# Layer 0's projections bound in issue order to the hops of each head's scan

## The chip, the core and the metric

The kernel runs on one NeuronCore of a Trainium2 chip. The metric is the device time of one execution in microseconds (us). The kernel before took 2446.84 us in the median of three runs (2445.88 to 2450.79).

## What is computed

A decoder step of two layers over 1024 prompt tokens and 8 x 8 sample tokens, 1088 columns in all, with a model width of 1024. Layer 0 is a gated DeltaNet mixer with 8 heads of 128 x 128, layer 1 a dilated window attention. The change lies in layer 0 alone. For each head the input is projected to q, k and v, each passes a causal convolution of 4 taps and a SiLU, and then the prompt's 16 chunks of 64 tokens (the kernel takes 8 chunks of 128) go through a recurrence:

```python
def causal_conv_silu(u, buf, w):
    ...
    for i in range(1, CONV_W):
        y = y + ext[:, i:i + L] * w[i]
    return jax.nn.silu(y), ext[:, L:]

def gated_delta_rule(q, k, v, g, beta, S0):
    ...
    sol = lax.linalg.triangular_solve(a_mat, rhs, left_side=True, lower=True, unit_diagonal=True)
    ...
    def step(S, xs):
        w_c, kcum_c, qk_c, qdec_c, kdec_c, gtot_c = xs
        u = w_c - jnp.einsum('bhck,bhkv->bhcv', kcum_c, S)
        o = jnp.einsum('bhck,bhkv->bhcv', qdec_c, S) + jnp.einsum('bhij,bhjv->bhiv', qk_c, u)
        S = S * gtot_c[..., None, None] + jnp.einsum('bhck,bhcv->bhkv', kdec_c, u)
        return S, o
```

## The kernel before

A framework schedules the program: the code calls the stages in an order, and a scheduler with a timeline of its own lays each engine's instructions in one line. `order_after(inst, first, reason)` (L116) adds a dependency that binds the issue order alone and has no semaphore. Between two instructions of TensorE (PE) it says that the one stands behind the other in PE's line.

`project()` (L121) makes one projection tile: three chunks of columns (384, 384 and 320), each of 24 products at L128 into one PSUM tile `pp`: 8 tiles of the width, times three pairs of a high and a low part (`whi`, `wlo` of the weights, `hh`, `hl` of the input). That is 72 products for a tile. Its callback does the convolution on ScalarE (ACT) and VectorE (DVE, `ca` at L72).

Layer 0's work on a head has four stages.

- `stage_k(h)` (L622) projects k and forms the chunk's triangular system `MT`: the decay `DT` is fetched from DRAM (L643), eight products at L655 give `kk`. The system's diagonal blocks of 32 x 32 go through DRAM into another layout (L696, L699, tile `Mi`), where DVE inverts them in a loop of 31 steps, each a product at L710 (`vtmp`) and a sum at L712 (`Vi`). The widths grow to 256. The result goes through DRAM once more (L714 `vsc`, L719 `Vt`).
- `stage_qv(h)` (L722) projects q and v.
- `stage_inverse(h)` (L759) builds the inverse of 128 x 128 out of these blocks: PE groups at L766, L773, L777, L782, L786 and L790 with copies on ACT and DVE between them, then L809 and L810 and the scaling at L812, which leave `kT` and `vn` ready for the scan.
- `stage_scan(h)` (L820) is a chain over the 8 chunks. The first chunk has one product on the chain, L899 (`sc<-vn,kdec`), and a copy at L904. Each of the 7 others has two: L896 (`sc<-S,kT`), then `w` on DVE, then L899 (`sc<-w,kdec`), then `S` on DVE. These 15 products of a head are its hops, listed in `head["hops"]`. The outputs at L907, L910 and L832 lie beside the chain.

The main loop goes over h, with scan(h), then qv(h+1), k(h+2) and inverse(h+1) issued behind it, so that the projections of later heads fill the chain's gaps as the scheduler thinks fit. Heads 6 and 7 have no such projections left or only some; there the gate projections `gate()` stand behind the scan. Those of head 7 are bound by `behind` (L935): their product n goes behind hop (n - 54) // 16.

Of the kernel before, what the change touches and what calls it, by code (L numbers as in the profile page):

```python
# [22 lines left out]
NH = 8  # L23
# [19 lines left out]
def kernel(ctx, tc, I, O):  # L43
# [70 lines left out]
    def order_after(inst, first, reason):  # L114
        tc.add_manual_dep(inst.ins, first.ins.name,
                          mybir.DependencyInfo(mybir.DependencyClass.NoSync, mybir.DependencyReason.SCHED_ONLY),  # L116
                          reason=reason)

    newest = [None]

    def project(w, hh, hl, cb, chunks=CHUNKS, each=None):  # L121
        whi, wlo = w
        for ci, (c0, cn) in enumerate(chunks):
            acc = pp.tile([P, 512], F32, name="pp")
            n = 0
            for k in range(KD):
                for a, b in ((whi, hh), (whi, hl), (wlo, hh)):
                    mm = PE.matmul(acc[:, :cn], lhsT=a[:, k, :], rhs=b[k][:, c0:c0 + cn],  # L128
                                   start=(n == 0), stop=(n == 3 * KD - 1))
                    if each:  # L130
                        each(mm)
                    n += 1
            newest[0] = mm
            cb(ci, acc)
# [275 lines left out]
    def gate(pool, wsrc, h, hh, hl, done, zo="zo", zt="zt", bufs=3, each=None):  # L410

        w = wsplit(wraw(wsrc))
        def load(ci):
            oT = pool.tile([P, 384], F32, name="zo", tag=zo, bufs=bufs)
            SY.dma_start(out=oT[:, :CHUNKS[ci][1]], in_=oscr[h][:, CHUNKS[ci][0]:sum(CHUNKS[ci])])
            return oT
        tiles = [load(0)]

        def cb(ci, acc):
            c0, cn = CHUNKS[ci]  # L420
            cs = slice(c0, c0 + cn)
            oT = tiles[0][:, :cn]
            if ci < 2:
                tiles[0] = load(ci + 1)
            th = pool.tile([P, 384], F32, name="zt", tag=zt, bufs=bufs)
            A.activation(out=th[:, :cn], in_=acc[:, :cn], func=AF.Tanh, scale=0.5)
            stt(th[:, :cn], th[:, :cn], 1.0, acc[:, :cn], ALU.add, ALU.mult)
            stt(oT, th[:, :cn], 0.5, oT, ALU.mult, ALU.mult)
            done(ci, cs, oT)
        project(w, hh, hl, cb, each=each)  # L430

    def z_split(h, oh, ol):
        def done(ci, cs, oT):
            A.copy(out=oh[h][:, cs], in_=oT)  # L434
            (G if ci == 1 else V).tensor_tensor(out=ol[h][:, cs], in0=oT, in1=oh[h][:, cs].bitcast(F32),  # L435
                                                op=ALU.subtract)
        return done
# [18 lines left out]
    def slot(name, dtype=F32, shape=None):  # L456
        t = big.tile([P, 9 * P if name[:2] == "vn" else 8 * P if name == "DT1" else T], dtype, name=name)
        return t[:, :8 * P].rearrange("p (c n) -> p c n", n=P) if shape else t
# [87 lines left out]
    def conv_tile(t, dst):  # L546
# [3 lines left out]
        def cb(ci, acc):  # L550
# [34 lines left out]
            else:  # L585
                stt(dst[:, c0:NP], th[:, :256], 1.0, ca[:, :256], ALU.add, ALU.mult)
                v1 = th[:, 259:347].rearrange("p (b x) -> p b x", x=11)[:, :, 0:8]
                v2 = ca[:, 259:347].rearrange("p (b x) -> p b x", x=11)[:, :, 0:8]
                stt(sview(dst[:, NP:]), v1, 1.0, v2, ALU.add, ALU.mult)
        project(w, hh, hl, cb)  # L590
        if t != 8:
            ada.pump(1)
# [334 lines left out]
    heads = [{} for _ in range(NH)]  # L927

    def stage(f, h):
        if h < NH:  # L930
            f(h, heads[h])
# [5 lines left out]
    def behind(mm):  # L937
# [2 lines left out]
            order_after(mm, heads[-1]["hops"][hop], "leaves room for the chain of the scan")  # L940
        count[0] += 1

    stage(stage_k, 0)
    stage(stage_qv, 0)
    stage(stage_k, 1)
    stage(stage_inverse, 0)
    for h in range(NH):
        stage(stage_scan, h)
        stage(stage_qv, h + 1)
        stage(stage_k, h + 2)  # L950
        stage(stage_inverse, h + 1)
        for i in GATED.get(h, ()):
            def store(ci, cs, oT, i=i):
                SY.dma_start(out=oscr[i][:, cs], in_=oT)
            a, b = PLACE[i]
            if i == 2 and h == NH - 1:
                oT = slot("vT")
                SY.dma_start(out=oT, in_=oscr[2])
            if i != 2 or h == NH - 1:
                oh[i], ol[i] = slot(a, F32R)[:, :T], slot(b, F32R)[:, :T]  # L960
            if i == 2 and h == NH - 1:
                A.copy(out=oh[2], in_=oT)
                G.tensor_tensor(out=ol[2], in0=oT, in1=oh[2].bitcast(F32), op=ALU.subtract)
                continue
            gate(sb, W0[:, 3072 + i * P:3072 + (i + 1) * P], i, hh, hl, store if i == 2 else z_split(i, oh, ol),
                 "xin", "ca", 2, behind if h == NH - 1 else None)
    ada.pump(100)

    l0b.close()
# [12 lines left out]
    def out_project(pool, layer, wout, resid, x1, oh, ol, post, chunks=CHUNKS):  # L982
        a, b = chunks[0][0], sum(chunks[-1])
        for j in range(KD):
            w = wsplit(wraw(wout[:, j * P:(j + 1) * P]))
            xr = pool.tile([P, WIDE], F32, name="xr", bufs=2)[:, :b - a]
            SY.dma_start(out=xr, in_=resid[j][:, a:b])
            gt = GTm[layer]

            def cb(ci, acc):  # L990
                c0, cn = chunks[ci]
                n = min(cn, NP - c0)
                stt(x1[j][:, c0:c0 + n], acc[:, :n], gt[:, j, 0:1], xr[:, c0 - a:c0 - a + n], ALU.mult, ALU.add)
                if n < cn:
                    s = sview(x1[j][:, NP:])
                    V.tensor_tensor(out=s, in0=sview(acc[:, n:cn]), in1=bc(gt[:, j, 1:9], NL), op=ALU.mult)
                    V.tensor_tensor(out=x1[j][:, NP:], in0=x1[j][:, NP:], in1=xr[:, NP - a:], op=ALU.add)
            project(w, oh, ol, cb, chunks)
            sq = pool.tile([P, WIDE], F32, name="sq", bufs=2)[:, :b - a]
            A.activation(out=sq, in_=x1[j][:, a:b], func=AF.Square)  # L1000
            if j == 0:
                qs = sq
            else:
                V.tensor_tensor(out=sq, in0=sq, in1=qs, op=ALU.add)
                qs = sq
            post(j)
        return qs
# [444 lines left out]
    for hp in range(4):  # L1452
        smd, vnew = [None] * NG, [None] * NG
        nmd = sd.tile([P, 4], F32, name="nmd", bufs=2)
        for g in (2, 1, 0):
            qTs, kTs, vTs = (sb.tile([P, 2, NS], F32, name=n, bufs=3) for n in ("qTs", "kTs", "vTs"))
            for a in range(2):
                h = 2 * hp + a
# [105 lines left out]
```

## Time and profile before

| | us |
|---|---|
| median of three runs | 2446.84 |
| the profiled execution's own time | 2428.75 |
| its span | 2427.0 |
| PE busy | 2282.0 |
| DVE busy | 1376.6 |
| ACT busy | 941.6 |
| GpSimd (POOL) busy | 260.4 |

The span runs from the first to the last instruction of the profiled execution. A matmul of float32 shows as two records, a product of L128 as one. The granted clock of PE (PEclk) is a share of full speed: 1.00 is 2.4 GHz, 0.50 is 1.2 GHz.

### The profile page before, as it was taken

The page shows a single profiled execution, that of the slowest core. Times are in us where ns is not written, and L with a number is a line of the kernel's source. Part 1 is how long each engine was busy: PE and PEld are TensorE (multiplying, and loading weights), DVE is VectorE, ACT ScalarE, POOL GpSimd, SP SyncE. Part 2 cuts the span into 40 slices and gives each one's busy share as a digit, 9 for nine tenths or more (in the row PEclk, how much of TensorE's full clock was granted, in tenths as well). Part 3 has the DMA queues.
Part 4 walks back from the last instruction along what each step waited for, and adds up shares of the span by engine and source line. Part 5 has one row for each costly group of instructions (what it writes and reads, how often), then busy time and mean ns, then how long its engine had stood idle before and what let it go on. Part 6 is the DMA issues. An engine that isn't in the chain of part 4 may idle for free.

```text
span 2427.0 us, 43290 instructions
## 1 busy us (share of the span) xinstructions
PE 2282.0 (94%) x16647; PEld 2147.1 (88%) x16647; DVE 1376.6 (57%) x3414; ACT 941.6 (39%) x2477; POOL 260.4 (11%) x418
## 2 busy tenths in 40 slices
PE   7799999999999999899999999899998999999997
PEld 5688788779889898799988999899998999999897
DVE  6678767866875437327643374633737337375334
ACT  6445444444544324333233432334323333225234
POOL 3213222222321102200000000000000000000000
PEclk9889889888989999799999999999999999999999
DMA  9223223233223355439732497744967349785634
GB/s 324 62 68 91 63 74 84 60 73 79 79 77 97 88 158 165 131 84 335 228 109 74 132 345 204 237 115 125 351 197 249 115 122 340 198 288 169 213 103 148
DMA packets 482255, 379.42 MB, mean 156 GB/s; under 512 B 46206, under 2 KB 457071, under 8 KB 482048
## 3 DMA queue, kind: packets, MB, share of 16 engines
q1 hardware_dynamic: 482048, 376.65, 51.4%
q8 instruction: 131, 2.15, 0.4%
q14 instruction: 76, 0.62, 0.1%
HBM read 322.31 MB, written 54.27 MB: 155 GB/s over the span
## 4 chain that ended last, share of the span: by engine, by line
PE 67%; DMA 13%; DVE 9%; issue 6%; ACT 3%; POOL 1%; SPq 1%; POOLq 0%; ACTq 0%; DVEq 0%
PE pp L128 46%; DMA DT<-gcscr 2%; PE ps L1182 2%; PE ps L1200 2%; DMA qb<-qscr 2%; PE sc L1400 2%; DVE pr L1351 1%; DMA kc<-in_cache_kv_w_dram 1%; DMA wraw<-in_a_w_in_dram 1%; PE ps L1146 1%; DMA out_kv_s_dram<-knew 1%; PE ps L1191 1%; DMA aw<-in_ada_w_dram 1%; PE ps L150 1%; DMA out_y_p_dram<-yn 1%
## 5 line engine op out<-in xcount | busy, mean ns | idle before, releaser
L128 PE MATMUL pp<-hh,whi 128*128 128x384 f32 (+1 forms) x2688 | 915.2, 341 | 12.2 <-DVE vT L1140 4.2
L128 PE MATMUL pp<-hl,whi 128*128 128x384 f32 (+1 forms) x2688 | 906.1, 337 | 1.3 <-POOL hl L211 1.3
L128 PE MATMUL pp<-hh,wlo 128*128 128x384 f32 (+1 forms) x2688 | 901.5, 336 | 1.2 <-DVE wlo L111 1.2
L128 PEld LDWEIGHTS pp<-hh,whi 128*128 128x128 f32 x2688 | 514.0, 191 | 25.5 <-DVE vT L1140 6.6
L128 PEld LDWEIGHTS pp<-hl,whi 128*128 128x128 f32 x2688 | 514.6, 191 | 9.1 <-issue 4.6
L128 PEld LDWEIGHTS pp<-hh,wlo 128*128 128x128 f32 x2688 | 512.9, 191 | 6.3 <-issue 2.7
L111 DVE TENSOR_TENSOR wlo<-wraw,whi 128x1024 fp32r<-128x1024 f32 x136 | 170.2, 1251 | 127.7 <-ACT whi L110 126.9
L110 ACT CAST whi<-wraw 128x1024 fp32r<-128x1024 f32 x144 | 150.6, 1046 | 235.2 <-PE pp L128 146.2
L1187 ACT ACTIVATE sm<-sm,stg 128x128 f32<-128x128 f32 (+1 forms) x192 | 86.6, 451 | 359.8 <-DVE stg L1185 317.5
L1351 DVE TENSOR_TENSOR pr<-kc,qb 128x1024 f32<-128x1024 f32 x128 | 154.9, 1219 | 89.9 <-DMA qb<-qscr 56.2
L1341 DVE TENSOR_REDUCE ST<-pr 128x8 f32<-128x1024 f32 x128 | 153.7, 1214 | 1.1
L435 POOL TENSOR_TENSOR ol<-zo,oh 128x384 fp32r<-128x384 f32 x9 | 9.2, 1017 | 1302.6 <-ACT oh L434 1285.7
L72 DVE SCALAR_TENSOR_TENSOR ca<-xin,cwT,ca 128x384 f32<-128x384 f32 (+1 forms) x216 | 130.4, 608 | 7.6 <-ACT ca L577 6.2
L1185 DVE CUSTOM_DVE_ANT_0 sm<-ps,mA 128x256 f32<-128x256 f32 (+1 forms) x128 | 48.3, 377 | 137.1 <-PE ps L1182 136.2
L1200 PE MATMUL ps<-vnat,pT 128*128 128x128 f32 x560 | 96.3, 279 | 4.4 <-DVE pT L1196 4.4
L710 DVE TENSOR_TENSOR vtmp<-Vi,Mi 128x2 f32<-128x2 f32 (+30 forms) x248 | 95.7, 386 | 4.4 <-PE ps L690 0.7
L1182 PE MATMUL ps<-kT,qT 128*128 128x128 f32 (+1 forms) x384 | 93.3, 324 | 3.8 <-DVE stg L1185 3.6
L1200 PEld LDWEIGHTS ps<-vnat,pT 128*128 128x128 f32 x560 | 85.6, 189 | 10.6 <-ACT pTn L1380 4.2
L1194 ACT COPY pT<-ps 128x256 f32<-128x256 f32 (+1 forms) x96 | 32.4, 337 | 114.7 <-PE ps L1191 113.5
L128 PE MATMUL pp<-oh,whi 128*128 128x384 f32 (+1 forms) x216 | 72.0, 333 | 2.7 <-DVE zt L72 2.7
L72 DVE SCALAR_TENSOR_TENSOR hh<-pp,GT,xr 128x384 f32<-128x384 f32 (+1 forms) x48 | 27.3, 571 | 83.0 <-PE pp L128 79.2
L1185 DVE CUSTOM_DVE_ANT_0 sm<-ps,mG 128x128 f32<-128x128 f32 x64 | 18.4, 288 | 98.6 <-PE ps L1182 69.1
(449 smaller groups left out, 3681.5 us busy)
## 6 DMA issues: line engine op xcount, KB each, us to landing
qb<-qscr SPq DMA_DIRECT2D x128, 512.0 KB
kc<-in_cache_kv_w_dram SPq DMA_DIRECT2D x104, 512.0 KB
vc<-in_cache_kv_w_dram SPq DMA_DIRECT2D x104, 512.0 KB
wraw<-in_b_w_in_dram SPq DMA_DIRECT2D x80, 512.0 KB
wraw<-in_a_w_in_dram SPq DMA_DIRECT2D x32, 512.0 KB
wraw<-in_ada_w_dram SPq DMA_DIRECT2D x24, 512.0 KB
stgc<-gscr SPq DMA_DIRECT2D x32, 260.0 KB
aw<-in_ada_w_dram SPq DMA_DIRECT2D x8, 1024.0 KB
```

Source lines behind the costliest of these rows:

```text
L72: return (eng or V).scalar_tensor_tensor(out=out, in0=in0, scalar=scalar, in1=in1, op0=op0, op1=op1)
L110: A.copy(out=hi, in_=raw)
L111: (eng or V).tensor_tensor(out=lo, in0=raw, in1=hi.bitcast(F32), op=ALU.subtract)
L128: mm = PE.matmul(acc[:, :cn], lhsT=a[:, k, :], rhs=b[k][:, c0:c0 + cn], start=(n == 0), stop=(n == 3 * KD - 1))
L710: V.tensor_tensor(out=tv, in0=Vi[:, :na, :w], in1=Mi[:, :w, c].unsqueeze(1).broadcast_to([P, na, w]), op=ALU.mult)
L1182: PE.matmul(sv, lhsT=qT[:, b * P:(b + 1) * P], rhs=kT[:, k0:k0 + w], start=True, stop=True)
L1185: V.tensor_tensor_reduce(out=sm[:, :w], in0=sv, in1=mk, scale=1.0, scalar=3e38, op0=ALU.add, op1=ALU.min, accum_out=stg[:, b, 128:129])
L1187: A.activation(out=sm[:, :w], in_=sm[:, :w], func=AF.Exp, scale=-1.0, bias=stg[:, b, 128:129], accum_out=stg[:, b, 129:130])
L1200: PE.matmul(ob[:, (b % 4) * P:(b % 4 + 1) * P], lhsT=pT[:, i * P:(i + 1) * P], rhs=vnat[:, k0 // P + i, :], start=(i == 0), stop=(i == w / ...
L1341: V.tensor_reduce(out=sv[:, n:n + 4, :], in_=pr.rearrange("p (n a e) -> p n a e", a=2, e=P), op=ALU.add, axis=AX.X)
L1351: V.tensor_tensor(out=out, in0=k, in1=q, op=ALU.mult)
L1400: mm = PE.matmul(od[32 * j:32 * j + 8, f * P:(f + 1) * P], lhsT=Z[g][:, a * NB + 2 * j + c, 8 * k:8 * k + 8], rhs=vc[:, j, a * P:(a + 1) * P],
```

## The change

`project()` gets a list of functions, `paced`, that each of its products is passed to when the caller gave none. `along(h)` makes such a function for head h: the product n of the projections issued beside that scan goes behind hop (n - 24) // 14 from n = 24 on (for head 6: (n - 48) // 24 from 48 on), and every later one behind the last hop at the latest. The list is set anew behind each `stage_scan(h)` and emptied at the end of the layer. Nothing is computed otherwise.

```diff
+    paced = []
+
     def project(w, hh, hl, cb, chunks=CHUNKS, each=None):
...
-                    if each:
-                        each(mm)
+                    for f in [each] if each else paced:
+                        f(mm)
                     n += 1
...
+    def along(h):
+
+        n, hops = [0], heads[h]["hops"]
+        step, free = (24, 48) if h == NH - 2 else (14, 24)
+
+        def each(mm):
+            if n[0] >= free:
+                order_after(mm, hops[min(len(hops) - 1, (n[0] - free) // step)], "along the chain of the scan")
+            n[0] += 1
+        return each
+
...
     for h in range(NH):
         stage(stage_scan, h)
+        paced[:] = [along(h)]
         stage(stage_qv, h + 1)
         stage(stage_k, h + 2)
         stage(stage_inverse, h + 1)
...
+    paced.clear()
     ada.pump(100)
```

The scheduler lays all engines anew with these bounds, up to the end of layer 0. In the changed program the lines from L122 on stand 2 further down.

PE, the inverse of the head to come: before, it is laid between the hops of the running head. Here L773 and L777 are groups of the inverse of head 3, L907, L910 and L832 outputs of head 2's scan, L664, L667 and L677 the sample tokens' system.

```order
L664 MATMUL ps<-tri_s,gall 64x64
L773 MATMUL lv<-VT,MT_3926 32x32 x4
L907 MATMUL sc<-S,qT_3391 128x128
L773 MATMUL lv<-VT,MT_3926 32x32 x4
L667 MATMUL ps<-kT_4806 64x64
L910 MATMUL sc<-w,DT_2860 128x128
L777 MATMUL lv<-Vt_4095,Aw 32x32 x7
L832 MATMUL sc<-ident,o 128x128
```

Now, behind the last hop of head 1 (the first row), the whole inverse of head 2 follows (from the last row on), with no product of L128 up to the first hop of head 2.

```order
L901 MATMUL sc<-w,kdec 128x128
L909 MATMUL sc<-S,qT_2328 128x128
L834 MATMUL sc<-ident,o 128x128
L912 MATMUL sc<-w,DT_1797 128x128
L573 MATMUL pp<-ident,cst 27x128
L834 MATMUL sc<-ident,o 128x128
L602 MATMUL ps<-ident,kT_3741 128x128 x2
L602 MATMUL ps<-ident,kT_3741 64x128
L657 MATMUL ps<-kT_3741 128x128 x8
L666 MATMUL ps<-tri_s,gall 64x64
L669 MATMUL ps<-kT_3741 64x64
L768 MATMUL lv<-ident,Vt_3031 128x128 x8
```

The inverse of a head stood between the hops of the head before it, and stands behind them after heads 1, 3 and 5.

DVE, the end of the inversion loop (`vtmp`, `Vi`): before, its last step is over while `w` and `S` of the same head are still to come.

```order
L710 TENSOR_TENSOR vtmp<-Vi,Mi 128x256
L72 SCALAR_TENSOR_TENSOR ca<-xin,cwT,ca 128x384
L831 TENSOR_SCALAR o<-o,so 64x128
L712 TENSOR_REDUCE Vi<-vtmp 128x8
L111 TENSOR_TENSOR wlo<-wraw,whi 128x1024
L167 TENSOR_SCALAR SH_96<-ps,vecs 128x9
L72 SCALAR_TENSOR_TENSOR w<-sc,bp,vn_3737 128x128
L72 SCALAR_TENSOR_TENSOR ca<-xin,cwT,ca 128x384 x3
L705 MEMSET Vi 32x8 x4
L72 SCALAR_TENSOR_TENSOR S<-S,egt,sc 128x128
```

Now the last `S` of head 1 (the first row) stands ahead of the loop's last five steps, of widths 196 to 256.

```order
L72 SCALAR_TENSOR_TENSOR S<-S,egt,sc 128x128
L833 TENSOR_SCALAR o<-o,so 128x128
L803 TENSOR_TENSOR kdec<-kN,kd 128x512
L712 TENSOR_TENSOR vtmp<-Vi,Mi 128x196
L111 TENSOR_TENSOR wlo<-wraw,whi 128x1024
L714 TENSOR_REDUCE Vi<-vtmp 128x7
L72 SCALAR_TENSOR_TENSOR o<-sc,rq,t_3376 128x128
L575 COPY cso<-pp 27x128
L72 SCALAR_TENSOR_TENSOR ca<-xin,cwT,ca 128x344
L72 SCALAR_TENSOR_TENSOR ca<-xin,cwT,ca 128x384
L712 TENSOR_TENSOR vtmp<-Vi,Mi 128x203
```

The loop's last sum stands 28 rows behind that `S`, where the last five `w` and the last five `S` of its head stood behind it.

## Rows read from the trace of the kernel before

**Rows 1.** The page: the engines' busy time over the span

```profile
PE 2282.0 (94%) x16647; PEld 2147.1 (88%) x16647; DVE 1376.6 (57%) x3414; ACT 941.6 (39%) x2477; POOL 260.4 (11%) x418
```

**Rows 2.** Windows, first hop to next: PE, PEld, DVE, ACT, POOL busy; PEclk; DMA share, GB/s

```profile
193.00:264.00 71.00, 67.87 (x569) 59.01 (x568) 54.38 (x163) 32.65 (x102) 24.50 (x30) 0.90 0.31 79
264.00:351.40 87.40, 81.29 (x605) 71.34 (x605) 65.47 (x201) 42.04 (x137) 23.80 (x41) 0.90 0.30 74
351.40:441.00 89.60, 83.84 (x603) 72.50 (x603) 64.96 (x200) 42.06 (x137) 23.86 (x41) 0.88 0.27 71
441.00:528.30 87.30, 82.59 (x605) 72.75 (x604) 65.85 (x204) 41.84 (x137) 22.70 (x40) 0.87 0.28 73
528.30:619.90 91.60, 88.15 (x636) 78.49 (x635) 64.94 (x202) 45.44 (x155) 25.47 (x47) 0.87 0.31 74
619.90:697.90 78.00, 73.53 (x574) 64.11 (x573) 59.20 (x188) 37.35 (x121) 20.28 (x35) 0.93 0.30 78
697.90:784.40 86.50, 85.77 (x628) 78.66 (x626) 58.05 (x156) 38.26 (x110) 15.48 (x25) 0.96 0.33 92
784.40:840.00 55.60, 53.38 (x316) 48.77 (x315) 25.93 (x65) 19.81 (x56) 12.37 (x15) 0.94 0.27 78
```

**Rows 3.** Windows, PE alone: length, busy (records), PEclk, DMA share, GB/s; around head 2's end

```profile
375.00:420.00 45.00, 44.02 (x375) 0.99 0.31 77
420.00:425.00 5.00, 5.00 (x35) 0.50 0.44 119
...
445.00:450.00 5.00, 5.00 (x21) 0.53 0.25 60
```

**Rows 4.** PE by line and form, head 6: count | busy us, mean ns | idle us

```profile
L128 PE MATMUL pp<-hh,whi 128*128 128x384 f32 x72 | 25.5, 354 | 0.0
...
L128 PE MATMUL pp<-hh,wlo 128*128 128x320 f32 x34 | 11.0, 324 | 0.0
```

**Rows 5.** PE in order of time: start, duration; ends of runs of 20 and 22 products, then two neighbours

```profile
376.62 0.33 PE L128 MATMUL pp<-hl,whi 128*128 128x384 f32 x1
...
379.94 0.34 PE L128 MATMUL pp<-hh,wlo 128*128 128x384 f32 x1
...
363.12 0.31 PE L128 MATMUL pp<-hh,wlo 128*128 128x320 f32 x1
...
366.20 0.31 PE L128 MATMUL pp<-hh,wlo 128*128 128x320 f32 x1
...
447.56 0.52 PE L128 MATMUL pp<-hh,wlo 128*128 128x384 f32 x1
447.88 0.52 PE L128 MATMUL pp<-hh,whi 128*128 128x384 f32 x1
```

**Rows 6.** DVE in order of time: head 2, the last step and the last scaling

```profile
399.26 0.42 DVE L712 TENSOR_REDUCE Vi<-vtmp 128x8 f32<-128x256 f32 x1
...
431.66 0.68 DVE L812 TENSOR_TENSOR vn<-lv,bp 128x512 f32<-128x512 f32 x1
```

**Rows 7.** DVE by line and form, 351.4 to 441: convolution, decay, last loop step

```profile
L72 DVE SCALAR_TENSOR_TENSOR ca<-xin,cwT,ca 128x384 f32<-128x384 f32 x18 | 11.0, 611 | 0.8 <-ACT ca L577 0.6
L72 DVE SCALAR_TENSOR_TENSOR DT<-DT,gc,mD 128x128 f32<-128x128 f32 x8 | 2.3, 345 | 4.5 <-DMA DT<-gcscr 4.5
...
L710 DVE TENSOR_TENSOR vtmp<-Vi,Mi 128x256 f32<-128x256 f32 x1 | 0.6, 634 | 0.0
```

**Rows 8.** PE in order of time, the start of head 3's inverse

```profile
410.42 0.82 PE L766 MATMUL lv<-ident,Vt 128*128 128x128 f32 x6
```

**Rows 9.** All engines in order of time, head 0's inverse ahead of the scan

```profile
154.60 0.41 DVE L712 TENSOR_REDUCE Vi<-vtmp 128x8 f32<-128x256 f32 x1
...
161.68 0.86 PEld L766 LDWEIGHTS lv<-ident,Vt 128*128 128x128 f32 x7
```

**Rows 10.** SyncE's line: the trip through DRAM in head 2

```profile
399.71 1.80 SPq L714 DMA_DIRECT2D vsc<-Vi  x4
...
403.57 3.42 SPq L719 DMA_DIRECT2D Vt<-vsc  x4
```

## The prediction

> **What bounds the kernel now.** I read the page first, then windows from head to head, then PE and DVE in order of time around the hand-over from one head to the next. The page shows that PE is busy for 2282 of the 2427 us of the span and DVE for 1377 [rows 1]. So PE bounds the whole, and in the stretch that the change touches, layer 0's eight scans, it does too: the windows give 647 us for them, of which PE is busy for 616 [rows 2]. The reader should see two losses there. PE idles for about 31 us, and its granted clock is 0.87 to 0.96 of full. The clock's loss has a place. In head 2 the clock is 0.99 while hops and projections are mixed, and 0.50 in the stretch behind, where PE is just as busy but has few or no projections left between the last hops and the next head's inverse [rows 3]. A product of 384 columns comes every 0.175 us in the first kind of stretch and every 0.32 us in the second [rows 5]. That is what the change goes for: in heads 1 to 3, seven of a head's last eight hop intervals have no projection product, so the head's first half has all of them and its second half none.
>
> **The change, part by part.** The work on PE stays the same. By the order of both programs it is only laid elsewhere, from layer 0's first scan to head 7's last hop. Behind that point PE, DVE, ACT and SyncE hold the same instructions in the same order, so I price that section alone and take everything else as zero.
>
> *Prices.* A projection product costs 0.175 us with 384 columns (3.32 us over 19 steps) and 0.147 with 320 (3.08 over 21) [rows 5], on average 0.166. In head 6, PE has hardly a gap (85.77 busy of 86.5) [rows 2]. It makes 3 x 72 products of 384 and 3 x 34 of 320 columns [rows 4], which is 37.8 + 15.0 = 52.8 us. The remaining 33.7 us fall on 176 other matmuls, hops included: **0.191 us each**, at a clock of 0.96. It is the densest head, and the one whose make-up comes nearest to that of the changed order, so I take that price.
>
> *Hop stretches.* With 14 products behind each hop an interval is 2.3 us of products and some 9 others, 1.7 us. By the changed order, from a head's first hop to its last: head 0 has 199 products and 169 others, 65.3 us; head 1, 216 and 142, 63.0; heads 2 and 4, 210 and 169, 67.1 each; head 3, 216 and 145, 63.6; head 5, 230 and 145, 65.9; head 6, 279 and 175, 79.7.
>
> *Tails with products.* Behind the last hop of heads 0, 2, 4 and 6 there are 17, 6, 6 and 33 products with 23, 20, 20 and 2 others: 7.2, 4.8, 4.8 and 5.9 us.
>
> *Bare tails.* Behind heads 1, 3 and 5 stands the whole inverse of the next head, some 108 matmuls, and no product before the next head's first hop (10 products behind head 5, 1.7 us). They wait on a chain that the new DVE order starts late:
> - DVE has 33 instructions from the last `S` to the last `Vi`, convolution steps of 0.61 us and loop steps of up to 0.63 among them. Their durations in the trace sum to 15.5 us. Neighbours overlap by 0.07 (eight of 0.345 us are busy for 2.3) [rows 7], so 12.5 to 13; I take 13.
> - The trip through DRAM: from the end of the last `Vi`, 399.68 [rows 6], over `vsc` and `Vt` [rows 10] to the first transpose at 410.42 [rows 8] took 10.7 us, and 6.7 ahead of head 0 (155.01 to 161.68) [rows 9]. I take 10, near the one that is inside a scan, with SyncE's line as full as it will be.
> - The inverse itself took 21.9 us, from 410.42 [rows 8] to the end of `vn`, 432.34 [rows 6], with hops in between and 10 us of it or less at half clock [rows 3]. Bare and at full clock I put it between 17 and 21.9 and take 18, since the hops fall away and its hand-overs stay.
>
> That makes 41 us (36 to 46). Nothing covers it: the next head's products stand behind its first hop in PE's line. Behind such a tail the clock should be low, as at 445 us [rows 3]: the 24 free products cost 24 x 0.145 = 3.5 us more, with the others 4. So 45 us for each of the three tails.
>
> *Both ends.* 47 products that stood ahead of head 0's first hop stand behind it now, so this hop comes 7.8 us earlier, at 185.2 instead of 193.0. In head 7, 54 products and 17 others come on top: 12.2 us by price. Its 55.6 us [rows 2] hold waits, since 224 products and 48 others cost 46.4 by price. So between 58.6 (all waits covered) and 67.8; I take 65, because the intervals with the waits, those of 3 us, keep their make-up.
>
> *Sum.* 185.2 + (65.3 + 7.2) + (63.0 + 45) + 71.9 + (63.6 + 45) + 71.9 + (65.9 + 1.7 + 45) + (79.7 + 5.9) + 65 = 881, where head 7's last hop stands at 840 now [rows 2]. That is **41 us later**. The profiled execution took 2428.75 us in all, 18 less than the median of the runs; against its own time the sum is 2470, and on the median of 2446.84 it is **2488**. With tails of 36 to 46 us, others at 0.183 to 0.20 us and head 7's bounds, this case reaches from +11 to +68, 2458 to 2515. The value of 0.183 comes from the stretch at 0.99, where 144 products leave about 21 us to 115 others [rows 3].
>
> On the trip through DRAM the Trainium skill, "DMA: Bandwidth & Descriptors", section "Anatomy of one DMA — SWDGE (gpsimd) path", gives a fixed cost of about 2 us for one transfer of small size. For two dependent ones that is an estimate of 4 us; the tail would be 35 us and the sum about +23. Both trips seen here took longer, and they decide.
>
> **The rivals.**
>
> *Faster: the even mix keeps the clock.* The half-clock stretches of now [rows 3] go, because products lie in every interval. If PE runs at full clock without gaps, the others cost less than head 6 shows: 86.5 x 0.96 less the idle 0.7 is 82.3 us, and less 52.8 that is 29.5 for 176, 0.168 each. On the 1114 others of the hop stretches this gives 26 us back. With tails at 36 (15 less), no slow start behind them (12) and head 7 at 58.6 (6), the sum is 41 - 59 = -18: 2429. It decides from about 6 us less per head (41 over seven heads). For it speaks the clock of 0.99 in the mixed stretch; against it, that the same stretch gives 0.183 for the others, and that three bare tails are new places for a low clock. The Trainium skill, "TensorE: Matmul & The Clock Gate", section "HAM oscillation — how this bites in real kernels", has the clock fall with gaps in PE's work and rise with contiguous work, which would favour this rival. The trace agrees in part only: the clock was 0.50 from 420 to 425, where PE was busy for all of 5 us.
>
> *Slower still: the hops wait for DVE.* Products now stand behind each hop, so a late `w` or `S` stops them too, where a free product could fill in before. The slack is 14 products, 2.3 us. It is used up when DVE has three or more convolution steps of 0.61 us [rows 7] in front of `w` or `S` (0.35 each). If one DVE instruction too many, 0.35 to 0.61 and 0.48 in the middle [rows 7], adds to each of the 15 hops of seven heads, that is 50 us: +91, 2538. For it: DVE is busy for 65 of 87 to 90 us per head [rows 2], and must do the same work in less. Against it: DVE's work, laid by the new order and priced by the trace's durations, comes to less than PE's in nearly all hop intervals.
>
> *No change: the parts cancel.* Tails at 36 us, no slow starts, others at 0.178: 41 - 15 - 12 - 14 = 0, 2447. It takes three of my choices to be wrong to the same side. That the change does nothing is excluded by the order.
>
> **How the numbers follow.** The forecast gets 0.54, the faster rival 0.20, the slower still 0.20, no change 0.06. A measurement can tell about 0.2%, 4.9 us, from no change. So faster by more than that: 0.20; within it: 0.06; slower: 0.74. The forecast's own range is 2458 to 2515. Taken out to half of the faster and nearly all of the slower rival, the range is **2434 to 2542**.
>
> **What would show it.** In the changed profile the first hops of heads 1 to 6 should follow each other at alternating distances, 72 and 108 us, instead of 78 to 92. Behind the last hops of heads 1, 3 and 5, PE should show some 41 us without L128's line, first waiting for DVE's last `Vi` and then, at the first transpose, for the DMA that fills `Vt`; the clock there should be near 0.50. In the hop stretches the clock should be 0.95 or more and an interval about 4 us. The forecast is wrong if the heads stay at equal distances (then DVE reached `Vi` in time and the tails are short), if a hop interval is well above 4 us with `w` or `S` as the releaser (the slower rival), or if the tails are there but the hop stretches are near 57 us (the faster one).

## The result and the profile after

The changed kernel takes 2511.13 us in the median of four runs (2508.53 to 2513.05), the kernel before 2446.36 beside it: slower, ratio 1.0267 with a 95% interval of 1.024 to 1.0295, or 65 us. The forecast was 2488 (41 us slower), with the range 2434 to 2542.

The page first: PE is as busy as before to 12 us, the span is 83 us longer [rows 1].

```profile
PE 2293.6 (91%) x16647; PEld 2152.7 (86%) x16647; DVE 1388.4 (55%) x3414; ACT 943.8 (38%) x2477; POOL 256.9 (10%) x418
```

The windows of the changed kernel from each head's first hop to the next one's, with the columns of [rows 2]:

```profile
189.60:262.80 73.20, 70.80 (x550) 62.60 (x549) 55.51 (x139) 37.81 (x118) 20.25 (x36) 0.97 0.24 64
262.80:376.90 114.10, 90.22 (x656) 78.55 (x656) 75.37 (x258) 46.44 (x157) 27.43 (x46) 0.82 0.29 71
376.90:451.10 74.20, 70.71 (x547) 62.47 (x546) 54.34 (x137) 36.37 (x114) 18.15 (x32) 0.97 0.23 62
451.10:573.40 122.30, 92.14 (x659) 79.06 (x659) 78.09 (x264) 47.36 (x161) 28.67 (x50) 0.80 0.27 67
573.40:648.50 75.10, 71.56 (x547) 63.16 (x546) 54.21 (x137) 36.36 (x114) 18.05 (x32) 0.96 0.23 61
648.50:764.70 116.20, 98.17 (x685) 84.92 (x685) 78.18 (x257) 49.10 (x170) 26.84 (x52) 0.83 0.25 66
764.70:849.20 84.50, 83.39 (x629) 76.53 (x629) 55.50 (x135) 36.79 (x101) 16.82 (x22) 0.99 0.29 79
849.20:911.00 61.80, 61.10 (x402) 56.12 (x401) 30.97 (x72) 23.45 (x60) 13.66 (x15) 1.00 0.33 96
```

The heads no longer take 78 to 92 us each but alternate between some 75 and 114 to 122. Head 7's last hop stands at 911 instead of 840, 71 us later. Behind it the same instructions in the same order took 1598.9 us instead of 1587. Over the profiles of this study that rest lies between 1587 and 1600, so these 12 us can't be put down to the change. The profiled execution before was also 18 us under the median of its kernel, so the 65 us between the medians are the better measure of the loss.

PE alone in windows (length, busy, clock, DMA share, GB/s): head 1's hops and its tail, head 3's hops and its tail, then the first hop interval of head 2 and of head 3.

```profile
262.80:331.50 68.70, 64.70 (x465) 0.98 0.29 79
331.50:376.90 45.40, 25.51 (x191) 0.60 0.30 60
451.10:526.60 75.50, 65.98 (x468) 0.95 0.29 72
526.60:573.40 46.80, 26.15 (x193) 0.55 0.25 59
376.90:382.00 5.10, 5.10 (x35) 0.92 0.00 0
451.10:465.60 14.50, 7.64 (x71) 0.79 0.26 37
```

The tails are there: 45 and 47 us with PE busy for little more than half, at a clock of 0.55 to 0.60. The reader should also see what was not forecast: the hop stretches of heads 1 and 3 are longer than 63 us, and head 3 loses 14.5 us in its first interval, with PE busy for 7.6.

A fourth bare stretch lies ahead of the scans. In the kernel before, PE made 455 products ahead of head 0's first hop, now 312: the other 143 come later, 71 of them in head 0 and 54 in head 7. Head 0's own inverse now stands there without a product, from 150 us to the first hop, where the kernel before had 130. PE in this stretch, before and now:

```profile
150.00:193.00 43.00, 39.49 (x323) 0.92 0.29 72
```

```profile
150.00:189.60 39.60, 24.64 (x189) 0.57 0.37 72
```

At the 0.166 us that the prediction takes for a product, 143 of them are 23.7 us of work. The first hop comes only 3.4 us earlier, so some 20 of the 71 us are lost here.

How a tail is made up, head 1's. DVE in order of time: the last `S`, a wait, the last `Vi`, and the `vn` that the next head's first hop needs.

```profile
331.94 0.34 DVE L72 SCALAR_TENSOR_TENSOR S<-S,egt,sc 128x128 f32<-128x128 f32 x1
...
343.14 1.40 DVE L72 SCALAR_TENSOR_TENSOR DT<-DT,gc,mD 128x128 f32<-128x128 f32 x5 [4.89 <-DMA DT<-gcscr]
...
349.88 0.42 DVE L714 TENSOR_REDUCE Vi<-vtmp 128x8 f32<-128x256 f32 x1
...
376.14 0.69 DVE L814 TENSOR_TENSOR vn<-lv,bp 128x512 f32<-128x512 f32 x1
```

PE in the same stretch: the inverse's first transposes wait for the DMA, as forecast, but for 0.9 us only.

```profile
345.28 0.47 PE L834 MATMUL sc<-ident,o 128*128 128x128 f32 x1 [10.14 <-DVE o L833]
...
356.88 1.61 PE L768 MATMUL lv<-ident,Vt 128*128 128x128 f32 x8 [0.89 <-DMA Vt<-vsc]
```

PE's longest wait of this tail is another one. For 10.1 us its line stands on the transposition of head 1's last output (L834), whose scaling `o` (L833, at 344.94) stands on DVE close behind the wait for DT shown above. In head 3's tail the same wait is 12.3 us; head 5's has no wait for DT, and there it is 0.2. Behind L834 come the transposes and products of the next head's system, which wait 1.7, 1.9 and 1.4 us in head 1's tail. So two strands lead to the inverse, over DVE's loop and DRAM and over PE's own line. In the tails of heads 1, 3 and 5 the first one ends last, by 0.8 to 0.9 us.

So from the end of the last `S` (332.28) it is 18.0 us to the end of the last `Vi` (350.30), 6.6 to the first transpose (356.88) and 19.9 to the end of `vn` (376.83). PE's windows of the first and the last of these three pieces:

```profile
332.30:350.30 18.00, 2.81 (x11) 0.62 0.40 70
...
356.90:376.80 19.90, 18.31 (x160) 0.51 0.23 58
```

In the last piece PE is busy nearly throughout, mostly with the inverse's small matmuls, at half clock.

Why the loop is late is seen on SyncE's line and on DVE. In the changed kernel head 2's system leaves for DRAM 15 us into head 1, and `Mi` is there 22 us into it, when DVE sets its diagonal:

```profile
278.00 1.81 SPq L698 DMA_DIRECT2D msc<-MT  x4
281.16 1.71 SPq L701 DMA_DIRECT2D Mi<-msc  x4
```

```profile
285.26 0.09 DVE L703 MEMSET Mi<- 128x32 f32 x1
...
300.14 0.16 DVE L712 TENSOR_TENSOR vtmp<-Vi,Mi 128x2 f32<-128x2 f32 x1 [1.31 <-PE ps L692]
```

The loop starts 15 us after that. What releases it is L692, the last product of the sample tokens' system: `vtmp` lies in the tile (tag `su`) that this system uses. Heads 4 and 6 lose 17 us there (481.0 to 498.0 and 677.5 to 694.8), the kernel before 5 to 8. This piece of the chain was not forecast, and no run here moves it by itself.

In the kernel before the system was away and its loads were issued in head 0, 23 us ahead of head 1's first hop at 264.0, and the loop started ahead of that hop, at 251.3:

```profile
234.29 2.87 SPq L696 DMA_DIRECT2D msc<-MT  x4
...
239.85 0.90 SPq L699 DMA_DIRECT2D Mi<-msc  x2
```

k's products are the last third of a head's 216, bound to its last hops, so the system is finished only in the next head. The loop then ends 50 us after its start at 300.1, and a head with 14 products per hop is over in 68. One long tail gives the next system time (head 3's loop starts in it, at 367.0), so only every second head has one.

### The profile page after: what moved, and what is told of

Its sections match the earlier page's. It is cut to its first block, busy times and chain, and to the rows that moved or that the text cites. A ratio compares the mean times of both kernels' runs of the same rounds, so it can differ in the third digit from the quotient of the medians.

```text
span 2509.9 us, 43232 instructions
## 1 busy us (share of the span) xinstructions
PE 2293.6 (91%) x16647; PEld 2152.7 (86%) x16647; DVE 1388.4 (55%) x3414; ACT 943.8 (38%) x2477; POOL 256.9 (10%) x418
## 4 chain that ended last, share of the span: by engine, by line
PE 62%; DMA 13%; DVE 12%; issue 6%; ACT 4%; POOL 1%; SPq 1%; POOLq 0%; ACTq 0%; DVEq 0%
PE pp L130 42%; DMA DT<-gcscr 3%; PE ps L1197 2%; PE ps L1215 2%; DVE pr L1366 2%; DMA qb<-qscr 2%; PE sc L1415 2%; DMA kc<-in_cache_kv_w_dram 2%; DVE vtmp L712 1%; DVE ca L72 1%; DMA wraw<-in_a_w_in_dram 1%; PE ps L1161 1%; DMA out_kv_s_dram<-knew 1%; PE ps L1206 1%; DVE ST L1356 1%
## 5 line engine op out<-in xcount | busy, mean ns | idle before, releaser
L1215 PEld LDWEIGHTS ps<-vnat,pT 128*128 128x128 f32 x560 | 85.6, 189 | 14.0 <-ACT pTn L1395 5.0
L712 DVE TENSOR_TENSOR vtmp<-Vi,Mi 128x2 f32<-128x2 f32 (+30 forms) x248 | 90.2, 364 | 7.3 <-PE ps L692 2.2
L130 PE MATMUL pp<-oh,wlo 128*128 128x384 f32 (+1 forms) x216 | 71.9, 333 | 1.3 <-DVE wlo L111 1.3
```

What stands on the lines that cost most here:

```text
L712: V.tensor_tensor(out=tv, in0=Vi[:, :na, :w], in1=Mi[:, :w, c].unsqueeze(1).broadcast_to([P, na, w]), op=ALU.mult)
L1215: PE.matmul(ob[:, (b % 4) * P:(b % 4 + 1) * P], lhsT=pT[:, i * P:(i + 1) * P], rhs=vnat[:, k0 // P + i, :], start=(i == 0), stop=(i == w / ...
```

## The experiments

Theory A is this: a chain from k's last product over the system, DRAM, the loop, DRAM and the inverse, which starts too late for a head that is now shorter. Theory B is the slower rival of the prediction: the hop stretches lose the time, because w and S come late on DVE and nothing free can fill in.

### e1: 20 products behind each hop

```diff
-        step, free = (24, 48) if h == NH - 2 else (14, 24)
+        step, free = (24, 48) if h == NH - 2 else (20, 24)
```

> Twenty products behind each hop instead of 14 (the first 24 free as before; head 6 unchanged), so that a head's 216 products end by its tenth hop and k's by then too. Theory A (the bare tails are the end of a chain that k's projection starts too late: k's last products, the system, DRAM, 31 loop steps on DVE, DRAM, the inverse, some 117 us in all, against a head of about 70): the loop now ends between the hops of the next head, no tail of about 45 us is left behind heads 1, 3 and 5, heads follow each other at 75 to 85 us, and the time is 2430 to 2465 us. Theory B (the time goes in the hop stretches, where the hops wait for w and S and nothing free can fill in): the products that end earlier leave the later hops bare again, the stretches are no shorter, and the time stays above 2490 us.

Measured: 2463.59 us, 48 less than the change, 1.0108 of the kernel before (1.0083 to 1.0132). The change was timed in another session, where the kernel before took 2446.36 us; beside e1 it took 2439.75. With each taken against the kernel before beside it, the difference is 41 us (in the same way 67 for e2, 72 for e3, 39 for e5). The windows of PE for head 1's hops and tail, and head 4's:

```profile
271.90:350.70 78.80, 71.35 (x494) 0.89 0.33 77
350.70:368.80 18.10, 11.72 (x89) 0.62 0.38 101
539.80:614.00 74.20, 69.15 (x503) 0.95 0.32 80
614.00:636.40 22.40, 15.18 (x112) 0.62 0.32 59
```

Behind heads 0 to 5 no tail of 45 us is left; these two are the longest. That is A. The heads are longer than A had them, 81 to 98 us, since the hop stretches grew: head 1's from 68.7 to 78.8, head 4's from 69.1 to 74.2.

### e2: k ahead of q and v

```diff
-        stage(stage_qv, h + 1)
         stage(stage_k, h + 2)
+        stage(stage_qv, h + 1)
         stage(stage_inverse, h + 1)
```

> The pace is that of the change (14), but in the loop k of head h+2 is projected ahead of q and v of head h+1, so k's products are the first 72 of a head and v's the last. Theory A: k's system is made in the first half of the head, its loop has more than one head's time, the 45 us tails go. What is late now is v, so each head has a tail with some 60 matmuls of the inverse and 7 to 11 products, about 20 us; heads of 80 to 88 us, time 2430 to 2470 us. Theory B: the hop stretches are bound as in the change and no shorter; time above 2490 us.

Measured: 2437.11 us, 74 less than the change, and 1.0004 of the kernel before (0.9978 to 1.003). The pace and its 14 products per hop are the same, only the order of two calls differs. Windows with the columns of [rows 2], head 2's hops and tail:

```profile
357.80:424.70 66.90, 65.96 (x492) 57.81 (x493) 51.00 (x160) 32.95 (x112) 19.46 (x38) 0.95 0.26 69
424.70:444.40 19.70, 12.48 (x116) 10.29 (x115) 13.99 (x42) 9.34 (x25) 2.57 (x5) 0.86 0.32 92
```

The hop stretch is as long as in the change (68 in head 2), the long tails are gone and one of 16 to 21 us stands behind each of heads 0 to 5, as A had it. B falls. The tails are not all of it: head 7's last hop comes 72 us earlier than in the change, and of these 35 lie behind the last hops and 33 in the hop stretches, 27 of them in heads 1, 3 and 5. In a tail of e2 DVE shows what is late next:

```profile
439.51 0.35 DVE L72 SCALAR_TENSOR_TENSOR DT<-DT,gc,mD 128x128 f32<-128x128 f32 x1 [5.18 <-DMA DT<-gcscr]
...
443.61 1.28 DVE L814 TENSOR_TENSOR vn<-lv,bp 128x512 f32<-128x512 f32 x2
```

DVE keeps to the order of its line. It waits 5.2 us for the load of a later head's decay, and the `vn` that the next first hop needs stands behind it and runs at 443.61, although its products on PE were done at 437.2.

### e3: half the inversion loop

```diff
-        for c in range(1, 32):
+        for c in range(1, 16):
```

> As the change, but the inversion loop makes 15 of its 31 steps and leaves out the 16 widest ones (part of the triangular inverse is left out). That takes some 14 us of DVE's work off each head's chain. Theory A: the tails behind heads 1, 3 and 5 (45.8, 47.1 and 38.4 us in the changed kernel) shrink by 14 us each at least, in sum the time falls by 45 to 110 us, to 2400 to 2466. Theory B: only what DVE's relief gives the hops, under 25 us in all, and the tails stay above 40 us.

Measured: 2432.86 us, 78 less than the change. PE's windows, head 1's hops and tail:

```profile
258.00:323.80 65.80, 64.17 (x474) 0.99 0.30 78
323.80:347.70 23.90, 15.88 (x144) 0.64 0.26 53
```

The tail behind head 1 halves, from 45.4 to 23.9 us, so the loop does stand on the chain, and the tails no longer alternate (13 to 26 us behind heads 0 to 5). The time is in A's range, but the tails alone don't make the gain. Head 7's last hop comes 72 us earlier: 20 of these lie ahead of head 0's first hop, as its own loop is shorter too and ends at 129.9 instead of 157.6, and 51 in the hop stretches. The tails behind heads 0 to 5 fall by some 25 us in sum, and the one behind head 6 grows by 24.

### e4: only head 6 bound

```diff
-        paced[:] = [along(h)]
+        paced[:] = [along(h)] if h == NH - 2 else []
```

> Only head 6 is bound (24 products behind each hop from the 48th on), heads 0 to 5 are as in the kernel before. Theory A: head 6 has no head behind it that needs k's system, so nothing is lost there: 2436 to 2452 us, the kernel before within its noise. Theory B: head 6's hops wait for DVE, its stretch grows by 7 us or more, 2453 us or above.

Measured: 2448.92 us, 1.0041 of the kernel before (1.0006 to 1.0075), in the range of A, though clear of the kernel before by its interval. The loss of the change lies in heads 0 to 5; binding head 6 costs some 10 us, 1.5 to 18 by the interval.

### e5: the change with the decay steps later

The second loss is now tested by itself. The eight steps on DVE that wait for the load of DT go behind the second `w` of the running scan:

```diff
-                stt(DT[:, c, :], DT[:, c, :], gc[:, c, h:h + 1], mD, ALU.subtract, ALU.min)
+                d = stt(DT[:, c, :], DT[:, c, :], gc[:, c, h:h + 1], mD, ALU.subtract, ALU.min)
+                if h > 1:
+                    order_after(d, heads[h - 2]["ws"][1], "behind the load of the decay")
...
+        ws = head["ws"] = []
...
-                stt(w, pa, bp[:, c:c + 1], vn[:, c, :], ALU.mult, ALU.add)
+                ws.append(stt(w, pa, bp[:, c:c + 1], vn[:, c, :], ALU.mult, ALU.add))
```

> The change, and DVE's decay steps (L72, DT) of head h+2 are bound in DVE's line behind the second w of head h's scan, so that DVE doesn't stand at the head's start waiting for the DMA that fetches DT. Theory C (a second loss beside the tails: in the changed kernel DVE waits 41.9 us for this DMA, 5 to 7 us at each of the heads' starts, and the vn and o behind it hold up the first hops, which took 10 to 14.5 us behind heads with a long tail instead of 5): the wait goes to under 5 us in all, the first intervals of heads 1, 3 and 5 fall to 6 to 8 us, 15 to 30 us less than the change, 2481 to 2496 us. The tails of about 45 us stay. Theory D (the DMA wait is covered, PE would wait for the clock or the inverse there anyway): within 6 us of the change, 2505 to 2517.

Heads 1, 3 and 5, whose first intervals are long, stand behind the short tails, not behind the long ones as this text has it.

Measured: 2465.56 us, 46 less than the change, and below C's range. Waits of DVE, in the change and here:

```profile
DVE DT L72 <- DMA DT<-gcscr: 41.9, 7, 7.2
```

```profile
DVE DT L72 <- DMA DT<-gcscr: 5.8, 1, 5.8
```

The windows of PE here, head 1's hops and tail, head 3's:

```profile
262.10:325.50 63.40, 63.06 (x465) 1.00 0.32 86
325.50:363.40 37.90, 25.16 (x190) 0.62 0.29 72
439.50:503.00 63.50, 63.23 (x468) 1.00 0.32 85
503.00:540.80 37.80, 25.26 (x192) 0.62 0.34 73
```

The wait cost in both places: 5 and 12 us of the hop stretches of heads 1 and 3, and 7.5 and 9 of the tails, where it stood in DVE's line ahead of `o` and of the loop's last steps (343.14 above). The first intervals of heads 1, 3 and 5 fall to 6.5 to 6.7 us. So C held in kind and was too small in size, and tails of 38 us stay, as A says.

### e6, e7: k first with the decay steps later, 14 and 20 products per hop

The edits of e2 and e5 together; e7 has the step of e1 as well.

> k ahead of q and v under the pace of 14, and the decay steps bound as in the run beside it. With k first the wait for DT stood in each head's tail (434.3 to 439.5 us in head 2), with vn of the next head behind it. Theory C: 5 to 8 us less in each of six heads, 30 to 48 us: 2390 to 2408 us, faster than the kernel before. Theory D: within 8 us of k first alone, 2429 to 2445 us.

> The same with 20 products behind each hop, so that v too is ready before the head ends; by the order the tails hold 32 to 52 matmuls and hardly a product, and two or three hop intervals per head have none. If what is late in the tails is v, they shrink further: 5 us less per head than at 14, 2360 to 2385 us. If the bare late hops cost as much (low clock, DVE's hand-overs), 2390 to 2410, the same as at 14.

Measured: 2426.25 us (0.9935 of the kernel before, 0.9904 to 0.9966) and 2424.64 (0.9915, 0.9881 to 0.9949). Both are faster than the kernel before, and both miss their ranges: the gain over e2 is 11 and 12 us, not 30 to 75. Windows of PE in e6, head 1's hops and tail:

```profile
268.50:344.30 75.80, 69.37 (x515) 0.95 0.31 77
344.30:356.70 12.40, 11.45 (x114) 1.00 0.52 83
```

The tail fell from 20 to 12 us as meant, and the hop stretch grew from 65 to 76. At the start of head 5, 588 to 612, where the second hop comes 10.3 us after the first, the waits of e6 name a new one, the weights:

```profile
ACT whi L110 <- DMA wraw<-in_a_w_in_dram: 7.5, 1, 7.5
DVE wlo L111 <- ACT whi L110: 7.0, 1, 7.0
```

DVE again stands in order behind something that isn't there yet. Whether that is all of the loss was not tried.

### e8, e11, e10, e12: the kernel before with the decay steps later

The edit of e5 on the kernel before, without any pace: behind the second `w` (e8, and once more e11), the third (`["ws"][2]`, e10), the first (`["ws"][0]`, e12).

> The kernel before, without any pace, with the decay steps bound the same way. There DVE waits 31.6 us for DT in seven waits, about 4.5 us per head, in a stretch where PE is busy. Theory C: part of it comes off, 10 to 30 us: 2412 to 2432 us. Theory D: no change, 2436 to 2450 us.

> The kernel before with the decay steps bound behind the second w, once more and with more rounds, on another job: 2395 to 2415 us, 1 to 2% under the kernel before. Nearer than 0.5% to it would say that the first measurement was a good draw.

> The kernel before with the decay steps bound behind the third w instead of the second. The load had landed by the second w already, so nothing more can come off DVE's wait, and the system is made a hop later: 2395 to 2420 us, the same as with the second w or a little more. A time near 2440 would say that the gain of the bound steps was luck of the order that the scheduler found, and not the wait.

> The same bound behind the first w. In the kernel before the first w of a head comes 12 to 21 us after its first hop, and the load takes about 10 us, so the wait is gone here too: DVE waits under 8 us for DT, and the time lies between 2398 and 2430 us, below the kernel before in any case. At 2436 or more the wait for DT would not be what the other two gained by.

| kernel | us | ratio to the kernel before (95%) |
|---|---|---|
| e8, second `w` | 2398.88 | 0.9835 (0.9785 to 0.9884) |
| e11, second `w` again | 2404.01 | 0.9818 (0.9792 to 0.9844) |
| e10, third `w` | 2425.39 | 0.9892 (0.9861 to 0.9923) |
| e12, first `w` | 2418.76 | 0.9885 (0.9856 to 0.9914) |

All four beat both kernels, e11 by 1.8% and 4.3%. DVE's wait of the kernel before and of e8:

```profile
DVE DT L72 <- DMA DT<-gcscr: 31.6, 7, 5.7
```

```profile
DVE DT L72 <- DMA DT<-gcscr: 5.6, 1, 5.6
```

The wait is gone in all four, and all four gain over 1%. They differ by some 20 us among each other with the same wait left, so the wait alone doesn't set the gain. The rest should lie in the layout that the scheduler found around the bound steps, which was not tested by itself. In e10, for one, 21 us lie between head 2's last hop and head 3's first, in e8 8. e8 lies 13 us below C's range and e10 5 above its own; e11 and e12 lie in theirs.

e5 and e8 were timed side by side, and neither has the wait for DT at the heads' starts: 2465.56 against 2398.88. So the pace costs 67 us without this wait, as much as the 65 between the two kernels that both have it. The wait raised both by about the same.

### e9: a loose pace for all heads

```diff
-        step, free = (24, 48) if h == NH - 2 else (14, 24)
+        step, free = 24, 48
```

with the edit of e5.

> The order of the change (q and v, then k), the decay steps bound, and for all heads the loose pace that head 6 has in the change: 48 products free, then 24 behind each hop, so that a head's products end by its eighth hop. Theory A: k's system is early enough, the loop ends by the fourth w of the next head, no bare tail of 38 us or more behind heads 1, 3 and 5; 2395 to 2425 us, near the kernel before with the same decay steps (2398.9). If a pace by itself gains over the scheduler's own order, it is below 2395; if it costs even then, above 2425.

Measured: 2437.8 us (0.9966, 0.9942 to 0.999), outside the range. The long tails are gone (2 to 14 us behind heads 0 to 6), as A says. But against e8 it is 39 us slower, 34 with each taken against the kernel before beside it: a pace costs here even where it makes no long tail. By the first hops, 18 us of the 36 up to the last hop are in head 0 (84 against 66) and 10 in head 6. The products account for most of it, as in the change. Head 0 has 71 of them more than in e8 and head 6 has 48 more, 11.8 and 8.0 us at 0.166. In e8 these 119 lay ahead of head 0's first hop, which without them comes only 5 us earlier.

## Why the prediction was right, step by step

The forecast case, a bare tail behind every second head, is what happened. Of its terms (here a stretch ends and a tail begins with the start of the last hop, in the windows above with its end):

| term | forecast | measured |
|---|---|---|
| first hop of head 0 | 185.2 | 189.6 |
| head 0 in all | 72.5 | 73.2 |
| heads 1, 3, 5: hop stretch | 63.0, 63.6, 65.9 | 68.2, 75.2, 77.8 |
| heads 1, 3, 5: tail | 45, 45, 46.7 | 45.8, 47.0, 38.4 |
| heads 2, 4 in all | 71.9, 71.9 | 74.2, 75.1 |
| head 6 in all | 85.6 | 84.5 |
| head 7 | 65 | 61.8 |
| last hop of head 7 | 881 | 911 |

**The price of the hop stretches held** where nothing else interfered. At 0.166 per product and 0.191 per other matmul the even heads come to 2 or 3 us of the forecast, and in e5, without DVE's wait, the stretches of heads 1, 3 and 5 took 63.0, 63.2 and 66.5 (its even heads with their tails 76, 3 to 4 over the forecast).

**The term that was left out** is DVE's wait for the load of DT. The prediction's row for these steps shows it, 4.5 us per head [rows 7], and the prediction took only their duration from that row. The DT tile of a later head becomes free when the ending head's last product on it is done, so the load is issued at the hand-over, and in the changed kernel DVE's line has its first reader right behind. Head 3's start: PE's last use of the tile (by head 2), SyncE's issue, DVE, and PE up to the second hop:

```profile
450.46 0.39 PE L912 MATMUL sc<-w,DT 128*128 128x128 f32 x2
```

```profile
450.88 0.38 SPq L645 DMA_DIRECT2D DT<-gcscr  x1
```

```profile
460.66 2.19 DVE L72 SCALAR_TENSOR_TENSOR DT<-DT,gc,mD 128x128 f32<-128x128 f32 x8 [7.16 <-DMA DT<-gcscr]
...
462.77 0.28 DVE L833 TENSOR_SCALAR o<-o,so 128x128 f32<-128x128 f32 x1
```

```profile
463.10 0.47 PE L834 MATMUL sc<-ident,o 128*128 128x128 f32 x1 [6.70 <-DVE o L833]
...
465.56 0.80 PE L898 MATMUL sc<-S,kT 128*128 128x128 f32 x2
```

From its issue to its first reader the load took 9.8 us. The scaling of head 2's last output stood behind that reader on DVE, PE's line stood 6.7 us on the transposition of this output, and the second hop behind it came 14.4 us after the first. Head 5 shows the same with 5.5 us. In head 1 it was the chain itself: DVE's copy of the first `S` (270.98) stood behind the wait. In the three odd heads this made the hop stretches 29 us longer than forecast, nearly the whole 30 us that the last hop is later than in the sum.

The sum set a changed kernel without this wait against a kernel before that was measured with it (by e8, e10, e11 and e12 its removal gave 20 to 45 us there). In e5, which has no such wait, head 7's last hop stands at 868, 13 us ahead of the 881 of the sum. So the nearness of 2488 to 2511 is in part luck: the wait made the kernel slower than the sum, the tails priced too long made it faster, and the range had been opened for other terms.

**The first hop of head 0** is near its forecast by luck, too. The prediction has 47 products moved behind it, the traces 143, and the hop was to come earlier by all that the moved products cost. By this rule it would have come 23.7 us earlier, at 169, and the sum would have been 865. It came at 189.6, since head 0's inverse then stood bare and at a clock of 0.57. The prediction saw this for heads 1, 3 and 5 and not here.

**The tail's parts** shifted among themselves. DVE took 18.0 us where 13 stood (15.5 less 33 times 0.07 is 13.2), 4.9 of it the same DT wait. DRAM took 6.6, the lower of the two rows and not the 10 taken. The inverse took 19.9 instead of 18, at half clock, where the step priced full clock. PE did not first wait for the last `Vi`, as the signs had it, but for `o`; in the second strand, over PE's line, the transposes stood behind the next system's products. The slow start of 4 us that was added there is hardly seen: head 2's first interval took 5.1 us at 0.92.

On the trip through DRAM, the Trainium skill ("DMA: Bandwidth & Descriptors", "Anatomy of one DMA — SWDGE (gpsimd) path") led to an estimate of 4 us for two transfers. That section is about transfers that GpSimd issues; the ones here are issued by SyncE. This case's traces have 6.6 to 10.7.

**The faster rival** had one thing right. With products in every interval the clock rises to 0.93 to 1.00 in the hop stretches, against 0.87 to 0.90 over heads 1 to 4 before [rows 2]. It did not decide, since the tails give it back: over the eight heads the clock is 0.90, where it was 0.91. The Trainium skill ("TensorE: Matmul & The Clock Gate", "HAM oscillation — how this bites in real kernels") says that gaps lower the clock. The tails as a whole agree with it, 0.55 to 0.62 with PE busy for 56 to 72% of them; the last piece of head 1's does not, 0.51 with PE busy for 18.3 of 19.9 us.

**The slower rival** saw that DVE would hold up the hops, but by the wrong mechanism. Not one instruction too many in front of each hop, but one wait for a DMA per head did it, at the start of heads 1, 3 and 5.

## What to carry to other kernels

When filler work is bound to a chain, ask of each filler what it feeds: the last one in line becomes the first link of the next round's chain, and its latency must fit into one round. Order the fillers by that latency (here, k ahead of q and v took 67 to 74 us off the change), not by the order of the program. Ask also what the fillers leave behind: held back for later, they left head 0's inverse bare. And on an engine that keeps to the order of its line, look for the row that waits for a DMA and see what stands behind it, on other engines too: to move eight steps behind the load's landing was worth 39 to 46 us in the changed kernel and 20 to 45 in the kernel before, while no pace tried here gained anything by itself. When you price a new order from clean prices, price the old one the same way, or take the waits of the old one over.

## What was not expected of the hardware

PE at 1.2 GHz was not only a matter of idle time. In the kernel before its clock was 0.50 in 5 us in which it was busy throughout [rows 3], with small matmuls, most of them the inverse's, and no projection product; by its records it had been busy for the whole 15 us ahead of them too. And the length of DVE's wait did not tell its worth: 36 us less of it took 39 to 46 off the changed kernel, and 25 to 26 us less took 20, 31, 41 and 45 off the kernel before. What stands behind the waiting instruction would explain this; no run here shows it by itself.
